# A weighted sum of two expert outputs: each partition owns 128 tokens in a row, weights in one DMA, one last store

## The chip, the cores and the metric

The kernel runs on one core of one Trainium2 chip. The metric is device time in microseconds of one execution; lower is better. The core has a vector engine (VectorE, DVE in the profile), a scalar engine (ScalarE, ACT), two more engines that matter little here, and a sequencer that only issues transfers (SyncE, SP). Transfers between main memory (HBM) and on-chip memory (SBUF, 128 partitions) run on 16 DMA engines, which are fed by one queue for SP (q1 in the profile) and one for ACT (q10).

## The reference

For 16 x 1024 = 16384 tokens there are the outputs of two experts, 512 numbers each, and two weights. The result is their weighted sum:

```python
batch, seq, hidden, n_experts, k = 16, 1024, 512, 8, 2
# expert_outputs: (batch, seq, k, hidden), combine_weights: (batch, seq, k), float32
weights = combine_weights[..., np.newaxis]
return np.sum(expert_outputs * weights, axis=2).astype(np.float32)
```

That is 64 MiB to read, 32 MiB to write and 128 KiB of weights.

## The kernel before

Every partition gets 128 tokens, worked on in 16 groups (the loop over `g`) of J = 8 tokens. A group's input tile `et` is 128 partitions x 8 tokens x 1024 numbers: 32 KB for a partition, 4 MB in all. Six such tiles exist (`bufs=6`), so the load of group g + 6 reuses the memory of group g, once that group's store has read it.

Which tokens a partition gets is decided by the helper `rows`. The first 120 x 128 tokens are dealt so that partition p has 120 tokens in a row. The last 8 x 128 tokens are dealt so that partition p has 8 in a row. So in groups 0 to 14 the rows of two neighbouring partitions lie 120 tokens apart in memory (480 KB for the input, 240 KB for the output), and group 15 is one contiguous block (rows 32 KB and 16 KB apart).

The weights lie in the tile `wt`. They are loaded by two DMAs on ACT's queue (line 53): one for the 120 tokens, one for the 8. Line 58 is a small ScalarE instruction that loads its function table early.

In each group:
- Line 64 (SP) loads `et`. All 16 loads are issued from SP, in order.
- In groups 0 to 14, line 69 (VectorE) multiplies the tile by the weights in place, line 70 adds the two halves into `ot` (the first half of the same tile), and line 71 (ACT's queue) stores `ot`, 16 KB for a partition in one run.
- In group 15 the work is done token by token, to be short at the end: line 78 (ScalarE) scales the first expert's output, line 81 (VectorE) multiplies the second by its weight and adds. After every second token line 89 (SP) stores two tokens of every partition. These are four stores, with 4 KB for a partition each.

The order in an engine is fixed when the kernel is built, by a scheduler that moves a few instructions. VectorE's last four line-69 and line-70 instructions come in pairs, and two line-78 instructions stand in ACT's queue ahead of the last two stores of line 71. Transfers signal their end through eight semaphores, used in turn. So a transfer may also wait until an older one with the same semaphore has landed. In the kernel before, the fifth and the sixth load wait in this way for the two weight transfers.

Of the kernel before, what the change touches and what calls it, by code (L numbers as in the profile page):

```python
# [1 line left out]

# [4 lines left out]


@with_exitstack
def kernel(  # L10
    ctx: ExitStack,
    tc: tile.TileContext,
    expert_outputs: bass.AP,
    combine_weights: bass.AP,
    out: bass.AP,
):

    nc = tc.nc  # L20
    b, s, k, h = expert_outputs.shape
    assert k == 2
    n = b * s
    P = nc.NUM_PARTITIONS
    per = n // P
    assert per * P == n
    J = 8
    main = per - J
    eo = expert_outputs.rearrange("b s k h -> (b s) (k h)")
    cw = combine_weights.rearrange("b s k -> (b s) k")  # L30
    o = out.rearrange("b s h -> (b s) h")

    def rows(x):

        a = x[0 : P * main, :].rearrange("(p t) f -> p t f", p=P)
        b = x[P * main : n, :].rearrange("(p t) f -> p t f", p=P)
        return lambda t, c: a[:, t : t + c, :] if t < main else b[:, t - main : t - main + c, :]

    eo, cw, o = rows(eo), rows(cw), rows(o)

    dt = mybir.dt.float32
    mult = mybir.AluOpType.mult
    add = mybir.AluOpType.add
    copy = mybir.ActivationFunctionType.Copy

    last = per // J - 1

    wpool = ctx.enter_context(tc.tile_pool(name="w", bufs=1))
    ipool = ctx.enter_context(tc.tile_pool(name="in", bufs=6))

    wt = wpool.tile([P, per * k], dt)
    for t, c in ((0, main), (main, J)):
        nc.scalar.dma_start(
            out=wt[:, k * t : k * (t + c)].rearrange("p (t k) -> p t k", k=k), in_=cw(t, c)
        )

    warm = wpool.tile([P, 1], dt)
    nc.scalar.activation(out=warm, in_=nc.const_aps.tensor(1.0, (P, 1), dt), func=copy)  # L58

    for g in range(per // J):  # L60
        et = ipool.tile([P, J, k * h], dt)

        ot = et.rearrange("p j f -> p (j f)")[:, 0 : J * h].rearrange("p (j f) -> p j f", f=h)
        nc.sync.dma_start(out=et, in_=eo(g * J, J))  # L64
        if g < last:

            wb = wt[:, g * J * k : (g + 1) * J * k].unsqueeze(2).to_broadcast([P, J * k, h])
            ek = et.rearrange("p j (k h) -> p (j k) h", k=k)
            nc.vector.tensor_tensor(out=ek, in0=ek, in1=wb, op=mult)  # L69
            nc.vector.tensor_tensor(out=ot, in0=et[:, :, 0:h], in1=et[:, :, h : 2 * h], op=add)  # L70
            nc.scalar.dma_start(out=o(g * J, J), in_=ot)  # L71
            continue


        for c0 in range(0, J, 2):
            for i in range(c0, c0 + 2):
                t = g * J + i
                nc.scalar.activation(  # L78
                    out=et[:, i, 0:h], in_=et[:, i, 0:h], func=copy, scale=wt[:, 2 * t : 2 * t + 1]
                )  # L80
                nc.vector.scalar_tensor_tensor(  # L81
                    out=ot[:, i, :],
                    in0=et[:, i, h : 2 * h],
                    scalar=wt[:, 2 * t + 1 : 2 * t + 2],
                    in1=et[:, i, 0:h],
                    op0=mult,
                    op1=add,
                )
            nc.sync.dma_start(out=o(g * J + c0, 2), in_=ot[:, c0 : c0 + 2, :])


# [1 line left out]
_INS = ['expert_outputs', 'combine_weights']  # L93
_OUTS = [((16, 1024, 512), 'float32')]


# [23 lines left out]
```

## Time and profile before

| what | value |
|---|---|
| median of 4 runs | 240.79 us (240.65 to 240.85) |
| the profiled execution | 240.84 us, of which 238.7 us are the profile's span |
| VectorE busy | 201.3 us (84%), 38 instructions |
| ScalarE busy | 6.6 us (3%), 10 instructions |
| moved | 100.80 MB in 5328 packets, mean 422 GB/s |
| line 69, multiply | 15 times 8689 ns |
| line 70, add | 15 times 4423 ns |
| line 64, load | 16 of 4096 KB, median 47.2 us from issue to landing |
| line 71, store | 15 of 2048 KB, median 24.8 us |
| line 89, last stores | 4 of 512 KB, median 8.0 us |
| line 53, weights | 120 KB, 12.6 us; 8 KB, 22.0 us |

How to read it: a transfer's time from issue to landing holds the time that it stands in its queue behind others. In the rows of a DMA queue, the share is the time that its packets took, as a part of the time of all 16 engines in the stretch shown. A row's bytes over that time therefore give the speed of one engine while it works for that queue. MB are millions of bytes there.

### The profile page before, as it was taken

How to read it: one execution, taken by the hardware profiler on the slowest of the kernel's cores; microseconds unless marked ns; L12 is line 12 of the kernel's file. 1: busy time of each engine (PE TensorE's matmuls, PEld its weight loads, DVE VectorE, ACT ScalarE, POOL GpSimd, SP SyncE). 2: the span in 40 equal slices, each digit the busy share in tenths (PEclk: the TensorE clock that was granted, in tenths of full speed). 3: DMA queues.
4: the chain of work that ended last, by engine and by line, in shares of the span. 5: the costliest groups of instructions: out<-in, count | busy, mean ns of one | idle time of the engine just before them, and what ended most of it. 6: DMA issues, size and time to landing. Idle time of an engine off the chain costs nothing.

```text
span 238.7 us, 177 instructions
## 1 busy us (share of the span) xinstructions
DVE 201.3 (84%) x38; ACT 6.6 (3%) x10; POOL 0.2 (0%) x4
## 2 busy tenths in 40 slices
DVE  0079999999999998979979799797918999899940
ACT  2000000000000000000000000000000000000620
POOL 0000000000000000000000000000000000000000
DMA  7999989999999999999999999999999999999997
GB/s 269 452 443 440 428 349 437 412 439 483 434 401 417 428 428 439 437 475 406 423 412 483 395 437 442 439 406 428 483 393 439 442 437 401 439 478 395 398 403 300
DMA packets 5328, 100.80 MB, mean 422 GB/s; under 512 B 720, under 2 KB 848, under 8 KB 1360
## 3 DMA queue, kind: packets, MB, share of 16 engines
q1 hardware_dynamic: 2880, 69.21, 67.9%
q10 hardware_dynamic: 2448, 31.59, 31.0%
HBM read 67.24 MB, written 33.55 MB: 422 GB/s over the span
## 4 chain that ended last, share of the span: by engine, by line
DMA 65%; DVE 29%; ACT 1%; ACTq 0%; DVEq 0%; issue 0%; SPq 0%
DMA et<-in_expert_outputs_dram 39%; DMA out_dram<-et 21%; DVE et L69 18%; DVE et L70 10%; DMA wt<-in_combine_weights_dram 5%; ACT et L78 1%; DVE et L81 1%; DVEq L115 0%; ACTq L115 0%; ACTq L71 0%; SPq L64 0%; DVEq L81 0%
## 5 line engine op out<-in xcount | busy, mean ns | idle before, releaser
L69 DVE TENSOR_TENSOR et<-et,wt 128x8192 f32<-128x8192 f32 x15 | 130.3, 8689 | 27.8 <-DMA et<-in_expert_outputs_dram 14.4
L70 DVE TENSOR_TENSOR et<-et 128x4096 f32<-128x4096 f32 x15 | 66.2, 4423 | 0.4
L78 ACT ACTIVATE et<-et,wt 128x512 f32<-128x512 f32 x8 | 5.1, 710 | 220.0 <-DMA et<-in_expert_outputs_dram 218.1
L81 DVE SCALAR_TENSOR_TENSOR et<-et,wt 128x512 f32<-128x512 f32 x8 | 5.6, 748 | 0.2
L58 ACT ACT_TABLE_LOAD x1 | 1.3, 1283 | 1.7 <-PEq L104 1.7
L58 ACT ACTIVATE warm<-const-float32-1.0 128x1 f32<-128x1 f32 x1 | 0.2, 202 | 0.0
L104 POOL MEMSET const-bfloat16-1.0<- 128x1 bf16 x1 | 0.1, 101 | 0.0
L104 POOL MEMSET const-uint8-127<- 128x1 uint8 x1 | 0.1, 101 | 0.0
L104 POOL MEMSET const-float32-0.0<- 128x1 f32 x1 | 0.1, 98 | 0.2 <-issue 0.2
L104 POOL MEMSET const-float32-1.0<- 128x1 f32 x1 | 0.1, 98 | 0.0
## 6 DMA issues: line engine op xcount, KB each, us to landing
et<-in_expert_outputs_dram SPq DMA_DIRECT2D x16, 4096.0 KB, 47.2
out_dram<-et ACTq DMA_DIRECT2D x15, 2048.0 KB, 24.8
out_dram<-et SPq DMA_DIRECT2D x4, 512.0 KB, 8.0
wt<-in_combine_weights_dram ACTq DMA_DIRECT2D x1, 120.0 KB, 12.6
wt<-in_combine_weights_dram ACTq DMA_DIRECT2D x1, 8.0 KB, 22.0
```

Source lines behind the costliest of these rows:

```text
L58: nc.scalar.activation(out=warm, in_=nc.const_aps.tensor(1.0, (P, 1), dt), func=copy)
L69: nc.vector.tensor_tensor(out=ek, in0=ek, in1=wb, op=mult)
L70: nc.vector.tensor_tensor(out=ot, in0=et[:, :, 0:h], in1=et[:, :, h : 2 * h], op=add)
L78: nc.scalar.activation(out=et[:, i, 0:h], in_=et[:, i, 0:h], func=copy, scale=wt[:, 2 * t : 2 * t + 1])
L81: nc.vector.scalar_tensor_tensor(out=ot[:, i, :], in0=et[:, i, h : 2 * h], scalar=wt[:, 2 * t + 1 : 2 * t + 2], in1=et[:, i, 0:h], op0=mul ...
L104: nc = _bacc.Bacc("TRN2", target_bir_lowering=False, num_devices=1)
```

## The change

Partition p now owns tokens 128 p to 128 p + 127 for all 16 groups. Rows of neighbouring partitions lie 128 tokens apart in every load and store (512 KB for the input, 256 KB for the output). The weights come in one DMA, 1024 bytes for a partition, issued from SP ahead of the loads. Group 15 stores its eight tokens with one DMA after the last of them. The arithmetic is the same, instruction for instruction. In the built kernel, VectorE's order and that of ScalarE's arithmetic are as before; ACT's queue has two transfers fewer at its start; SP has one more at its start and one instead of four at its end. SP's first five loads now wait for nothing, and the sixth waits for the landing of load 0.

```diff
-    main = per - J
-    eo = expert_outputs.rearrange("b s k h -> (b s) (k h)")
-    cw = combine_weights.rearrange("b s k -> (b s) k")
-    o = out.rearrange("b s h -> (b s) h")
-
-    def rows(x):
-
-        a = x[0 : P * main, :].rearrange("(p t) f -> p t f", p=P)
-        b = x[P * main : n, :].rearrange("(p t) f -> p t f", p=P)
-        return lambda t, c: a[:, t : t + c, :] if t < main else b[:, t - main : t - main + c, :]
-
-    eo, cw, o = rows(eo), rows(cw), rows(o)
+    eo = expert_outputs.rearrange("b s k h -> (b s) (k h)").rearrange("(p t) f -> p t f", p=P)
+    cw = combine_weights.rearrange("b s k -> (b s) k").rearrange("(p t) k -> p (t k)", p=P)
+    o = out.rearrange("b s h -> (b s) h").rearrange("(p t) f -> p t f", p=P)
...
-    for t, c in ((0, main), (main, J)):
-        nc.scalar.dma_start(
-            out=wt[:, k * t : k * (t + c)].rearrange("p (t k) -> p t k", k=k), in_=cw(t, c)
-        )
+
+    nc.sync.dma_start(out=wt, in_=cw)
...
-        nc.sync.dma_start(out=et, in_=eo(g * J, J))
+        nc.sync.dma_start(out=et, in_=eo[:, g * J : (g + 1) * J, :])
...
-            nc.scalar.dma_start(out=o(g * J, J), in_=ot)
+            nc.scalar.dma_start(out=o[:, g * J : (g + 1) * J, :], in_=ot)
...
-        for c0 in range(0, J, 2):
-            for i in range(c0, c0 + 2):
...
-            nc.sync.dma_start(out=o(g * J + c0, 2), in_=ot[:, c0 : c0 + 2, :])
+        for i in range(J):
...
+        nc.sync.dma_start(out=o[:, g * J : (g + 1) * J, :], in_=ot)
```

More of the change, by code (lines that the diff above doesn't have):

```diff
@@ L70 @@
             nc.vector.tensor_tensor(out=ot, in0=et[:, :, 0:h], in1=et[:, :, h : 2 * h], op=add)
-            nc.scalar.dma_start(out=o(g * J, J), in_=ot)
+            nc.scalar.dma_start(out=o[:, g * J : (g + 1) * J, :], in_=ot)
             continue
-        for c0 in range(0, J, 2):
-            for i in range(c0, c0 + 2):
[L77 to L89, printed above, removed]
+        for i in range(J):
+            t = g * J + i
+            nc.scalar.activation(
+                out=et[:, i, 0:h], in_=et[:, i, 0:h], func=copy, scale=wt[:, 2 * t : 2 * t + 1]
+            )
+            nc.vector.scalar_tensor_tensor(
+                out=ot[:, i, :],
+                in0=et[:, i, h : 2 * h],
+                scalar=wt[:, 2 * t + 1 : 2 * t + 2],
+                in1=et[:, i, 0:h],
+                op0=mult,
+                op1=add,
+            )
+        nc.sync.dma_start(out=o[:, g * J : (g + 1) * J, :], in_=ot)
 _INS = ['expert_outputs', 'combine_weights']
```

## The prediction, made before the changed kernel was run

> **What bounds the kernel now.** I read the page from part 2 downwards: which resource is never free, then how fast it works in each stage, and last what the end of the span waits for. First the slices and the queues of the page:
>
> ```profile
> DVE  0079999999999998979979799797918999899940
> ...
> DMA  7999989999999999999999999999999999999997
> ...
> q1 hardware_dynamic: 2880, 69.21, 67.9%
> q10 hardware_dynamic: 2448, 31.59, 31.0%
> HBM read 67.24 MB, written 33.55 MB: 422 GB/s over the span
> ```
>
> The DMA row is full from the second slice to the last but one. The two queues (q1 is fed by SP, with loads and the last stores; q10 by ACT, with weights and the other stores) take 67.9% + 31.0% = 98.9% of all 16 engines' time. VectorE has 201.3 us of work in 238.7 us, so 37 us of slack. The time is therefore bytes over the speed of one DMA engine, plus a short head and tail. A change counts only if it alters the speed at which an engine moves a packet, or leaves engines empty.
>
> So the second view is the DMA view cut to stretches. In each row: packets, MB, share of 16 engines. First the middle, 62 to 192 us (loads at 480 KB pitch, stores at 240 KB):
>
> ```profile
> q1 hardware_dynamic: 1296, 37.75, 67.2%
> q10 hardware_dynamic: 1280, 18.61, 33.4%
> ```
>
> One engine moves 37.75 MB / (0.672 x 16 x 130 us) = 27.0 GB/s on loads and 18.61 / (0.334 x 2080) = 26.8 GB/s on stores. Then 205 to 220 us, where q1 carries the last load, whose 128 rows of 32 KB lie one behind the other:
>
> ```profile
> q1 hardware_dynamic: 154, 4.19, 64.8%
> ```
>
> That is 4.19 / (0.648 x 240) = 26.9 GB/s, the same speed. The third stretch, 22 to 32 us, is the one where loads are slower:
>
> ```profile
> q1 hardware_dynamic: 137, 3.96, 99.0%
> ```
>
> 3.96 / (0.990 x 160) = 25.0 GB/s, at an unchanged pitch of 480 KB. So the engines can lose 8% without any change of layout. The trace doesn't say why. The fourth, 231 to 237 us, is the tail with the four last stores in 4 KB packets:
>
> ```profile
> q1 hardware_dynamic: 524, 1.95, 81.4%
> ```
>
> 1.95 / (0.814 x 96) = 25.0 GB/s. These packets cost 7% more than the 16 KB ones.
>
> Third view: the timeline of the end.
>
> ```profile
> 221.29 0.34 ACTq L71 DMA_DIRECT2D out_dram<-et  x1
> ...
> 223.94 5.77 DVE L81 SCALAR_TENSOR_TENSOR et<-et,wt 128x512 f32<-128x512 f32 x8
> 224.06 0.34 ACTq L71 DMA_DIRECT2D out_dram<-et  x1
> ...
> 225.57 4.50 SPq L89 DMA_DIRECT2D out_dram<-et  x4
> ```
>
> When the last load has landed (221.2 us), the stores of groups 13 and 14 are still to be moved, then the four quarters of group 15. The end is a queue of writes, not arithmetic.
>
> **Part 1, the pitch.** Loads go from rows 480 KB apart to rows 512 KB apart, stores from 240 to 256 KB, weights from 960 to 1024 bytes. Bytes, packet sizes (32 KB and 16 KB) and the number of large DMAs stay. Only the starting addresses of the 128 rows move, and with them which parts of memory the 16 engines ask at one moment. No row of this trace shows a strided tile at a power-of-two pitch: the last load has a pitch of 32 KB, but its tile is one contiguous 4 MB block. So bounds. The low end is zero: both the nearest pitch (480 KB, 27.0 GB/s) and the contiguous tile (26.9 GB/s) run at one speed. A gain is excluded for this term, since no stretch exceeds 27.0. The high end is the slowest stretch. All loads at 25.0 GB/s take 67.11 MB / (16 x 25.0) = 167.8 us instead of 67.11 / (16 x 27.0) = 155.3 us, +12.4 us; the same 8% on the stores' 33.55 / (16 x 26.8) = 78.2 us is +6.3 us. Both: +18.7 us. I take a third of the way for the loads, +4.1 us, since the two rows that are like in kind stand at the low end, while address bits that are all alike in 128 rows can only make engines meet more often. Stores are spaced half as far: half of that share, +1.0 us. Sum +5.1 us, with both ends kept.
>
> The Trainium skill ("DMA: Bandwidth & Descriptors", section "Latency and other measured facts") has a row that speaks against this change: copies with a row pitch of 512 KiB reached 207 GB/s per direction, where a padded pitch reached 214, and far less at 2 and 4 MiB; it calls the mechanism an inference. By its ratio (an estimate from that page) 3.4% would fall on the loads, 5.3 us, or on loads and stores, 7.9 us. No run here shows it.
>
> **Part 2, the weights.** Removed: two issues on ACT (0.90 us together, at 0.72 us) and 128 packets of 64 bytes. Added: one issue on SP ahead of all 16 loads. SP's issues take 0.33 us (median), the first or worst 0.77 us, so load 0 starts up to 0.33 to 0.77 us later. In that gap the engines move the weights, 8 packets each. Packets of 960 bytes took 44 ns (112 of them were 3.1% of 160 us in the stretch from 2 to 12 us), so 0.35 us that they no longer take between the loads' packets. Net 0 to +0.4 us of empty engines, or a gain of 0.1 us from the small packets gone. I take +0.1 us. VectorE's start hardly moves: it waited for the weights until 13.39 us, but load 0, which must land too, was 12.5 us from its issue at 0.73. Earlier or later by 0.5 us doesn't count, for the DMA engines are full then. ACT's table load moves up, and its next need is at 221 us.
>
> Semaphore waits move as well. Before, SP's fifth and sixth loads waited for the two weight transfers (19.9 us in the view of SP's waits); after, five loads go at once and the sixth waits for load 0. Cost nothing either way, as four loads are 16.8 MB, 39 us of work in the queue. If that cover were gone, each such wait would be empty engines.
>
> **Part 3, the last store.** Four issues on SP become one, of 128 packets of 16 KB. Transfer: 2.10 MB / (16 x 25.0) = 5.24 us becomes 2.10 / (16 x 26.8) = 4.89 us, -0.35 us. Against it, the store now waits for all eight L81 instructions (end 229.71 us) instead of the first pair. What hides this: the stores of groups 13 and 14, 4.19 MB or 9.8 us, which start no earlier than 221.3 + 0.7 (from the issue of load 0 at 0.73 us to the first bytes near 1.4 us) = 222.0 us and last until 231.8. The single store can move at 229.75 + 0.7 = 230.5 us. Cover 1.3 us; cost 0. Behind the waiting SP nothing is queued. If the cover is gone, the engines are empty for at most the 4 us between the first pair's store and the last.
>
> The Trainium skill ("SBUF — State Buffer", "The DMA setup-cost knee") charges about 2 us to every DMA. Three fewer would by that estimate save 6 us; the quarters here overlap, and 0.35 us is what their rows allow.
>
> **Sum**, against the profiled execution of 240.84 us (span 238.7 and 2.1 around it; the median of the runs, 240.79, is the same within 0.05): 240.84 + 5.1 + 0.1 - 0.35 = 245.7 us.
>
> **The rivals.**
> - **The pitch costs nothing.** For it: the rows at 27.0 and 26.9 GB/s, which hint that an engine's own limit binds. Against it: 16 engines now walk rows with identical low address bits. 240.84 - 0.25 = 240.6 us, no change. Chance 0.14.
> - **Faster: the slow early stretch goes away.** The slow rows at 22 to 32 us lie where the sixth load had been issued late, behind the second weight transfer. If that made them slow, one tile returns from 25.0 to 27.0 GB/s: 4.19 / (16 x 25.0) - 4.19 / (16 x 27.0) = 0.78 us. With a free pitch: 240.84 - 0.25 - 0.78 = 239.8 us. It decides only if the pitch costs under about 0.5 us. Against it: the slowness begins some 5 us after that issue, and nothing of the queue had run dry. Chance 0.12.
> - **The tail runs dry.** A free pitch, but the cover of 1.3 us is missing: up to 4 us, say 242 us. Chance 0.04.
>
> **How the numbers follow.** A slower load stream, between +0.8 us and the upper bound, has 0.70, with 245.7 us as its value. About 0.2% (0.48 us) is what a measurement of this kernel can tell from no change. Slower: 0.70 + 0.04 = 0.74; within 0.2%: 0.14; faster: 0.12. The range starts at 240.3 us, so as to hold the free pitch and leave out most of the faster case (about 0.1), and ends at 252 us, which is +11.4 us for the pitch, about 60% of the way to its upper bound; I leave about 0.1 above. Alone, the likeliest case reaches from 241.5 to 252 us.
>
> **What would show it.** Right: in the stretch 62 to 192 us the loads' packets take more than the 27.0 GB/s row says (near 26.3), DMA still full, and VectorE's idle time before L69's successor grows by some 5 us. At the end one store with 16 KB packets follows two others without a gap, and the chain ends about 9 us after the last L81's start. Wrong: the rows stand at 27.0 GB/s (pitch free), or go below 25.0 (the bound fails), or empty DMA slices show at the head or the tail, or stores slow while loads don't.

## The result: 0.11% above the kernel before

The changed kernel takes 240.92 us, the kernel before 240.75 us over all its runs. The ratio is 1.0011 (interval 1.0006 to 1.0016), so it is slower by about 0.26 us (0.17 us by the medians), half of what the prediction called the limit of no change. The forecast was 245.7 us. The profiled execution took 241.53 us, of which 239.5 us are the span. The other runs go from 240.55 to 241.64 us, so the profiled execution is not a typical one; it lies 0.6 us above the median.

The page of the changed kernel, the same rows as before:

```profile
DMA  7999999999999999999999999999999999999897
...
q1 hardware_dynamic: 2592, 69.34, 67.9%
q10 hardware_dynamic: 2160, 31.46, 30.7%
HBM read 67.24 MB, written 33.55 MB: 421 GB/s over the span
```

DMA is as full as before (98.6% of the engines' time against 98.9%). If the pitch had cost what was forecast, the same bytes would have taken more time. The DMA view cut to 62 to 192 us tells whether an engine got slower (packets, MB, share of 16 engines):

```profile
q1 hardware_dynamic: 1289, 37.52, 66.8%
q10 hardware_dynamic: 1282, 18.71, 33.6%
```

37.52 / (0.668 x 2080) = 27.0 GB/s on loads and 18.71 / (0.336 x 2080) = 26.8 on stores: the speeds of before, to the digit. By the packets of the traces, one of 32 KB took 1.213 us on the mean from 60 to 200 us, in both kernels. The early slow stretch, 22 to 32 us, is still there:

```profile
q1 hardware_dynamic: 132, 3.80, 97.5%
```

3.80 / (0.975 x 160) = 24.4 GB/s, against 25.0 before. The end, in the timeline:

```profile
222.54 0.72 ACT L64 ACTIVATE et<-et,wt 128x512 f32<-128x512 f32 x1 [220.32 <-DMA et<-in_expert_outputs_dram]
222.60 0.34 ACTq L59 DMA_DIRECT2D out_dram<-et  x1
...
225.28 5.77 DVE L67 SCALAR_TENSOR_TENSOR et<-et,wt 128x512 f32<-128x512 f32 x8
225.39 0.34 ACTq L59 DMA_DIRECT2D out_dram<-et  x1
...
231.08 0.35 SPq L75 DMA_DIRECT2D out_dram<-et  x1
```

The one last store is issued when the eighth sum is done, and the store of group 14 still occupies the engines then (its last part ends at 233.5 us). The beginning is later. In the view of waits, VectorE's first multiply waited 13.4 us for the weights; now it waits for load 0, and the longest wait is 14.3 us. Before, then after:

```profile
DVE et L69 <- DMA wt<-in_combine_weights_dram: 13.4, 1, 13.4
```

```profile
DVE et L57 <- DMA et<-in_expert_outputs_dram: 29.1, 9, 14.3
```

So VectorE starts 0.9 us later in these two executions, while the whole change costs about 0.26 us by the ratio. Something was lost at the head and something won at the tail.

The packets of the two traces, added up over the 16 engines, say where. The last byte moves at 238.4 us instead of 237.3. Until 13 us the engines stand empty for 0.4 us longer, and the first packets of the loads together take 0.2 us longer. At 28 to 33 us, where the first store joins, the slow packets cost 1.2 us instead of 0.8. The single last store wins 0.3 us. And there is a gap that the prediction doesn't have: between 215 and 228 us the engines are empty for 0.7 us, where it was 0.3. Group 13's store (the one issued at 222.60) stands in ACT's queue behind the first line-64 instruction, which waits for the last load. The last engine ends its part of that load at 222.18 us. The engines end the store of group 12, one after another, from 222.27 us on, and the first packets of group 13's store come at 223.45. In the kernel before the three times are 220.84, 221.71 and 222.13. Since this execution took 0.6 us more than the median, its trace doesn't tell how much of these losses a typical one has.

### The profile page after: what moved, and what is told of

Its sections match the earlier page's. It is cut to its first block, busy times and chain, and to the rows that moved or that the text cites. A ratio compares the mean times of both kernels' runs of the same rounds, so it can differ in the third digit from the quotient of the medians.

```text
span 239.5 us, 169 instructions
## 1 busy us (share of the span) xinstructions
DVE 201.3 (84%) x38; ACT 6.6 (3%) x10; POOL 0.2 (0%) x4
## 4 chain that ended last, share of the span: by engine, by line
DMA 65%; DVE 29%; ACT 1%; ACTq 0%; DVEq 0%; issue 0%; SPq 0%
DMA et<-in_expert_outputs_dram 43%; DMA out_dram<-et 22%; DVE et L57 18%; DVE et L58 10%; ACT et L64 1%; DVE et L67 1%; DVEq L101 0%; ACTq L101 0%; SPq L43 0%; ACTq L59 0%; SPq L52 0%; DVEq L67 0%; DVEq L57 0%
```

## The experiments

**One part at a time.** Two theories. A: the pitch is free, and the small loss is the weights' place at the head less the saving of the one store. B: the pitch itself costs the little that was lost. Four kernels take the change apart: the pitch alone in the kernel before; the changed kernel with its weights back on ACT; the last store alone in the kernel before; the changed kernel with four last stores.

```diff
# e1, in the kernel before
-        a = x[0 : P * main, :].rearrange("(p t) f -> p t f", p=P)
-        b = x[P * main : n, :].rearrange("(p t) f -> p t f", p=P)
-        return lambda t, c: a[:, t : t + c, :] if t < main else ...
+        a = x.rearrange("(p t) f -> p t f", p=P)
+        return lambda t, c: a[:, t : t + c, :]
# e2, in the changed kernel
-    nc.sync.dma_start(out=wt, in_=cw)
+    nc.scalar.dma_start(out=wt, in_=cw)
# e3, in the kernel before
-            nc.sync.dma_start(out=o(g * J + c0, 2), in_=ot[:, c0 : c0 + 2, :])
+        nc.sync.dma_start(out=o(g * J, J), in_=ot)
# e4, in the changed kernel
-        nc.sync.dma_start(out=o[:, g * J : (g + 1) * J, :], in_=ot)
+            if i % 2:
+                nc.sync.dma_start(out=o[:, t - 1 : t + 1, :], in_=ot[:, i - 1 : i + 1, :])
```

> The kernel before with the 512 KB pitch alone (weights still two transfers on ACT's queue, 960 and 64 bytes for a partition, four last stores). Theory A (the pitch is free; the +0.17 us of the whole change is a later head, about +0.5 us, less a shorter tail, about -0.35 us): 240.7 to 240.9 us, ratio 1.000, and 27.0 GB/s for an engine on loads from 62 to 192 us. Theory B (the pitch costs the little that was lost, the other parts cancel): 241.0 to 241.5 us, ratio 1.001 to 1.003. The prediction's own term would be 245.8 us.

> The changed kernel with its one weight transfer back on ACT's queue, beside load 0 instead of ahead of it. Theory A: the head gets its 0.5 us back and the tail keeps its gain, 240.3 to 240.5 us, ratio 0.998; load 0's first packets start at about 1.5 us instead of 2.0. Theory B: 240.9 us or more, as the pitch stays.

> The kernel before with one last store of 8 tokens instead of four of 2. Theory A: 128 packets of 16 KB instead of 512 of 4 KB save 0.35 us and nothing runs dry, 240.4 us, ratio 0.9985. Theory B, or a tail that waits: 240.75 us or more.

> The changed kernel with four last stores of 2 tokens again. Theory A: the saving of the tail is lost, 241.25 us, ratio 1.002. Theory B: 240.9 us, as the changed kernel, since the store would then be worth nothing.

| kernel | median, us | ratio to the kernel before, interval |
|---|---|---|
| e1, pitch alone | 241.16 | 1.0022 (1.0012 to 1.0033) |
| e2, changed, weights on ACT | 240.64 | 0.9992 (0.9983 to 1.0001) |
| e3, before, one last store | 240.20 | 0.9981 (0.9972 to 0.9990) |
| e4, changed, four last stores | 241.29 | 1.0030 (1.0018 to 1.0041) |

Neither theory holds alone. The pitch costs 0.22%, about 0.5 us (against A). The one store saves 0.19%, about 0.46 us (against B). The weights ahead of the loads cost 0.19% by the changed kernel against e2, and 0.08% by e4 against e1; the first difference is uncertain by about 0.1%, the second by about 0.15%. The traces show the place: load 0's first packet starts at 1.75 us in e2 and at 2.23 in the changed kernel. Three parts of 0.2 to 0.5 us, one of the other sign, make the 0.26 us.

And yet e1's loads run at full speed from 62 to 192 us:

```profile
q1 hardware_dynamic: 1294, 37.68, 67.1%
```

37.68 / (0.671 x 2080) = 27.0 GB/s. So where do its 0.5 us go?

**Where the pitch costs.** The table of stretches gives the mean over the first 11.6 us in which data moves (last number, GB/s). The kernel before, then e1:

```profile
1.40:13.00 11.60, 0.00 (x0) 1.49 (x2) 0.00 (x0) 1.00 1.03 417
```

```profile
1.40:13.00 11.60, 0.00 (x0) 1.49 (x2) 0.00 (x0) 1.00 1.01 400
```

17 GB/s less for 11.6 us are 0.2 MB, which take 0.46 us at the 432 GB/s of the full engines. That is rough, since the row counts whole packets by their starts, and 0.2 MB are six packets. The packets of the trace show it finer. The first engine begins load 0 at 1.73 us in the kernel before and 1.74 in e1; the last begins at 2.33 and at 2.64. The first packet takes 1.86 us on the mean before and 1.96 in e1, and the first of load 1 1.21 and 1.38; the others up to 28 us take 1.21 to 1.23. So load 1 ends 0.50 us later in e1, on the mean of the engines, and load 8 is still 0.41 us late: the loss of about 0.5 us comes at the head and doesn't grow. The engines also end their parts of a load further apart. This is the time between the first and the last engine's completion of one load, and the mean time of completion, worked out from the completion packets of the profiled executions:

```
us from the first to the last engine's end of    load 0   load 2   load 8   mean end of load 1   load 8
before                                            0.44     0.37     0.37       22.30             121.23
e3, before with one last store                    0.46     0.46     0.46       22.35             121.31
e1, pitch alone                                   0.93     1.78     1.78       22.80             121.64
changed kernel                                    1.13     1.59     1.59       22.83             121.97
e5, 512 KB pitch from load 4 on                   0.32     0.29     0.31       22.38             121.23
e6, 512 KB pitch in loads 0 to 3                  0.85     0.92     0.92       22.58             121.54
```

Theory C: the pitch costs where the engines start together; it sets them apart once, and from then on they don't hinder each other. Theory D: it costs a little all along. Two kernels with mixed pitches tell them apart (some loads read other tokens than they should):

```diff
+    wide = eo.rearrange("(p t) f -> p t f", p=P)
...
-        nc.sync.dma_start(out=et, in_=eo(g * J, J))
+        nc.sync.dma_start(out=et, in_=wide[:, g * J : (g + 1) * J, :] if g >= 4 else eo(g * J, J))   # e5; g < 4 in e6
```

> The kernel before, but the loads of groups 4 to 15 are addressed at 512 KB pitch and those of groups 0 to 3 at 480 KB as before (so some tokens are read for others; stores and weights as before). Theory C (the pitch costs only where 16 engines start together, in the first 32 us; it sets them apart in time and the distance stays until the end): as the kernel before, 240.6 to 240.9 us, and the 16 parts of a load land within 0.4 us of each other all the way. Theory D (the pitch costs a little all along): 12 of 16 loads are wide, so 241.0 to 241.2 us, and the distance grows with every load.

> The reverse: loads of groups 0 to 3 at 512 KB pitch, those of groups 4 to 15 as before (some tokens are read for others). Theory C: as with the pitch alone, 241.0 to 241.3 us, and the 16 parts of a load land 1 to 2 us apart from the first loads on. Theory D: 4 of 16 loads are wide, so 240.8 to 240.95 us, with a distance that doesn't grow after group 3.

e5, with 12 of 16 loads wide, is at 1.0004 (0.9994 to 1.0013): no loss that can be measured. e6, with only the first four wide, is at 1.0035 (1.0022 to 1.0048), 241.45 us, even above C's expectation of 241.0 to 241.3. The first stretch agrees, e5 first, then e6:

```profile
1.40:13.00 11.60, 0.00 (x0) 1.49 (x2) 0.00 (x0) 1.00 1.04 417
```

```profile
1.40:13.00 11.60, 0.00 (x0) 1.49 (x2) 0.00 (x0) 1.00 1.01 406
```

D is out: the interval of e6, from 241.26 us up, lies above D's 240.95, and in e5 the wide loads hardly spread the engines and come no later than before (121.23 us for load 8 in both). So the loss belongs to the first four loads, as C says, and by the completion times to their first packets. Two points of C aren't borne out. The parts of e6's loads end 0.85 to 0.92 us apart and not 1 to 2. And the distance isn't what makes later wide loads free: in e5 the engines stay within 0.3 to 0.4 us of each other, and the wide loads cost nothing. The trace of e6 is of an execution of 240.50 us. Its other four took 241.41 to 241.68 us, and no trace shows where they lost more than the 0.3 us that this one is late at the head. Why wide addresses make the first packets later (a shared part of memory that several engines ask at once is the obvious guess) was not shown.

**Is there a pitch that costs all along?** Two ladders, read by stretches. In e9 the stores go to a scratch tensor at 512 KB, then 1 MB, then 2 MB pitch. In e10 four tiles are copied to a scratch tensor and loaded from there at 1 and 2 MB.

```diff
# e9
-            nc.scalar.dma_start(out=o[:, g * J : (g + 1) * J, :], in_=ot)
+            m = (1 << 17, 1 << 18, 1 << 19)[g // 5]
+            w = g * J * h
+            lad = big[0 : P * m].rearrange("(p c) -> p c", p=P)[:, w : w + J * h]
+            nc.scalar.dma_start(out=lad.rearrange("p (j f) -> p j f", f=h), in_=ot)
# e10
+        src = lad(17 + g // 4, g % 4) if 4 <= g < 12 else eo[:, g * J : (g + 1) * J, :]
```

> The changed kernel whose stores of groups 0 to 14 go to a scratch tensor instead of the output: groups 0 to 4 at a pitch of 512 KB, 5 to 9 at 1 MB, 10 to 14 at 2 MB. If a power-of-two pitch costs nothing at these sizes, an engine moves 26.8 GB/s on stores in all three stretches. If the term that the prediction charged exists but begins above 512 KB, the stretch at 2 MB is slower by 10% or more (by the skill's row, 164 against 207, about 21%), and the one at 1 MB lies between.

> Four tiles are first copied to a scratch tensor (8 stores of 4 MB, at 1 and 2 MB pitch). Then the changed kernel runs with the loads of groups 0 to 3 and 12 to 15 at 512 KB pitch, groups 4 to 7 from the scratch at 1 MB, groups 8 to 11 at 2 MB (so these give other tokens' sums). If pitch is free: 27.0 GB/s for an engine on loads in all stretches. If the term begins above 512 KB: 27.0 at 512 KB, lower at 1 MB, and 24 GB/s or less at 2 MB.

e9, DMA view from 107 to 139 us, as the stores at 1 MB begin, and from 140 to 181 us, when they have been running for a while:

```profile
q1 hardware_dynamic: 284, 8.36, 72.0%
q10 hardware_dynamic: 276, 4.00, 29.2%
```

```profile
q1 hardware_dynamic: 407, 11.96, 67.8%
q10 hardware_dynamic: 399, 5.85, 33.3%
```

Loads drop to 8.36 / (0.720 x 512) = 22.7 GB/s in the first and are back at 11.96 / (0.678 x 656) = 26.9 in the second, at the same pitch. The stores themselves keep 26.8 in both. At 2 MB, 182 to 226 us, it is again the loads beside them that are slower, at 12.85 / (0.709 x 704) = 25.7 GB/s, and the stores keep 26.8:

```profile
q1 hardware_dynamic: 448, 12.85, 70.9%
q10 hardware_dynamic: 369, 5.47, 29.0%
```

e10, loads at 1 MB pitch from 185 to 230 us, then at 2 MB from 231 to 288 us:

```profile
q1 hardware_dynamic: 428, 12.65, 67.6%
```

```profile
q1 hardware_dynamic: 552, 16.35, 67.0%
```

12.65 / (0.676 x 720) = 26.0 GB/s at 1 MB, and 16.35 / (0.670 x 912) = 26.8 GB/s at 2 MB: next to nothing lost there, with four times the pitch of the change. At the end of e9 stores stand alone at 2 MB pitch, 229 to 241 us:

```profile
q10 hardware_dynamic: 281, 4.19, 97.5%
```

4.19 / (0.975 x 192) = 22.4 GB/s, 16% below the 26.8 that they have beside loads. Standing alone isn't the reason, for in the kernel before the stores that are alone from 221 to 226 us move 2.08 / (0.987 x 80) = 26.3 GB/s:

```profile
q10 hardware_dynamic: 143, 2.08, 98.7%
```

So wider pitches do cost, in some stretches and not in others: on the loads for a time after the stores' pattern changed, little on loads at 2 MB in a steady stream, most on stores alone at 2 MB. e9 fits neither of its two cases, as the stores at 2 MB are slower only where they stand alone. It took 250.07 us in its one run, so these stretches add up. e10 (372.19 us) does more work, and its time isn't comparable. The Trainium skill ("DMA: Bandwidth & Descriptors", section "Latency and other measured facts") gives 207 and 164 GB/s per direction for copies at pitches of 512 KiB and 2 MiB, where 214 is the full rate. The 22.4 GB/s here agrees with it in direction. The 27.0 of the loads at 512 KB and the 26.8 of loads and of stores at 2 MB in a mixed stream don't, and the measurement decides for this kernel.

**The slow stretch at 28 to 32 us.** It is in both traces and was one of the prediction's rivals. Is it the first write as such (e7: a small store near the start, on top of e3), or does it follow the first full store (e8: that store held back)?

```diff
# e7
+    first = wpool.tile([P, 64], dt)
+    nc.gpsimd.memset(first, 0.0)
+    scratch = nc.dram_tensor("scratch", [P, 64], dt, kind="Internal").ap()
+    nc.scalar.dma_start(out=scratch, in_=first)
# e8
+            if g == 0:
+                held = ot
+                continue
+            if g == 1:
+                nc.vector.tensor_copy(out=held[:, 0, 0:1], in_=ot[:, 0, 0:1])
+                nc.scalar.dma_start(out=o(0, J), in_=held)
             nc.scalar.dma_start(out=o(g * J, J), in_=ot)
```

> The kernel before with one last store, and a store of 128 x 256 bytes to a scratch tensor issued from ACT's queue near the start. If the slow packets at 28 to 32 us come from the first write to memory as such, they are gone there (0.7 us of all engines) and the time is 239.5 to 239.9 us. If they come from the first full store beside a full load stream, or from something at that time, they stay and the time is 240.2 to 240.4 us.

> The kernel before with its first store held back until group 1 is done, about 13 us later (a copy of one number for a partition from group 1 into group 0's output makes it wait, so one output number in a row is wrong). If the slow packets follow the first store, they move from 28 to 32 us to about 41 to 45 us. If they belong to the loads or the time, they stay at 28 to 32 us.

In e7 the slow packets stay, at 30 to 34 us. Its time is 1.0013 (1.0005 to 1.0021), slower than e3 without the small store, which nobody expected. The view of its timeline shows the place:

```profile
221.92 0.72 ACT L83 ACTIVATE et<-et,wt 128x512 f32<-128x512 f32 x1 [218.77 <-DMA out_dram<-et]
222.03 0.34 ACTq L76 DMA_DIRECT2D out_dram<-et  x1
```

It is the gap that the changed kernel's trace has. The view names a store as what released ACT's first work on group 15, but the semaphore for which ACT's queue waits there signals loads alone: the last load lands at 221.83 us, 0.9 us later than in e3. Group 13's store, queued behind on ACT, is issued at 222.03 us (221.00 in e3), its first packets come at 222.87, and the engines had ended the store of group 12 between 221.50 and 222.11. The engines are empty for 1.1 us there; in e3 they are not. Why one more small transfer near the start makes the last load land later was not shown.

In e8 the slow packets move to 41 to 46 us, with the store, and are weaker: the 32 KB packets from 20 to 60 us take 0.16 us for each engine more than 1.213 us apiece, against 0.76 in the kernel before. Its single run took 239.68 us. To see whether that is a gain, the hold was built so that the result stays the same (zero times a number of group 1 is added) and put on e3 and on the changed kernel:

```diff
+            if g == 1:
+                nc.vector.scalar_tensor_tensor(
+                    out=held[:, 0, 0:1], in0=ot[:, 0, 0:1], scalar=0.0, in1=held[:, 0, 0:1], op0=mult, op1=add
+                )
+                nc.scalar.dma_start(out=o(0, J), in_=held)
```

> The kernel before with one last store and its first store held back: group 0's store waits for group 1's sums (a VectorE instruction on one number for a partition that adds zero times a number of group 1 makes the wait, and the result stays the same). If the single run of e8 (239.68 us) showed a gain of the late first store, and the last store adds its 0.45 us: 239.1 to 239.5 us, ratio 0.994, slow packets moved to about 41 to 45 us. If e8 was a lucky run: 240.1 to 240.3 us, ratio 0.998, as with one last store alone.

> The same hold in the changed kernel. If the cost of the pitch lies in the first loads (theory C) and the joining of the first store is a cost of its own, then the hold gains the same as in the kernel before, about 0.7 us: 240.1 to 240.4 us, and the 16 parts of a load still land more than 1 us apart. If the pitch costs only when the stores join: more gain, 239.7 us or less, with 0.5 us between the parts.

e11 is at 239.57 us, 0.9947 (0.9935 to 0.9960): faster than both kernels, and 0.34% below e3. e12 is at 240.44 us, 0.9985 (0.9976 to 0.9994), 0.26% below the changed kernel. Both are a little above what was expected. The gain is the same within the intervals, and the parts of a load still end 1.23 us apart in e12. The slow packets cost 0.34 us in e11 (0.80 in e3) and 0.39 in e12 (1.17 in the changed kernel). So the joining of the first store is a cost of its own, apart from the pitch. The hold has a second effect: the last load lands some 5 us before the store of group 12 ends, so no gap arises there. In e3 there was none to close; in e12 part of the gain may come from that. The DMA view from 27 to 33 us shows the loads where the first store joins, the kernel before, and then e11, in which it is held back:

```profile
q1 hardware_dynamic: 63, 2.06, 92.3%
q10 hardware_dynamic: 16, 0.26, 10.2%
```

```profile
q1 hardware_dynamic: 95, 2.59, 100.0%
```

2.06 / (0.923 x 96) = 23.2 GB/s before, 2.59 / 96 = 27.0 in e11, where no store has begun. Why the loads slow down when the first store joins, and why less so 13 us later, stays open.

e11 also shows that the distance between the engines doesn't slow them. At 480 KB pitch its parts end 0.43 us apart up to load 3, and 1.66 us from load 6 on, after the held store has joined. That is as far as in e1, and e11 is the fastest of all kernels that were run more than once.

## Why the prediction was wrong, step by step

- **The bound** was right: DMA engines at 27.0 and 26.8 GB/s, full in both kernels but for the head, the very end and the gap before group 13's store.
- **Part 1, the pitch, is the step that failed.** It took a speed between 27.0 and 25.0 GB/s and charged it on every byte: +5.1 us. The runs showed 27.0 and 26.8 GB/s at the new pitch, which is the sign that the prediction had named for a free pitch. Its own rows stood at 27.0 and 26.9, and the 25.0 belonged to something else, the first store's joining, as e8 and e11 show. The sign was right, the size ten times too big: e1 measured +0.22%, 0.5 us, paid once at the head. The two rows of the trace at one speed for two pitches hinted that the engine's own limit binds. The prediction wrote this down for the rival and gave it 0.14.
- **Part 2, the weights**: +0.1 us forecast, with 0 to 0.4 as ends. Measured +0.2 us (e4 against e1) to +0.46 us (changed kernel against e2), from the middle of that span to just above its end.
- **Part 3, the last store**: -0.35 us forecast, -0.46 us (0.19%) measured in e3. The cover held: the store was issued at 231.08 us and the engines were busy with group 14's store until 233.5. The gap before group 13's store, 0.3 us in the trace before and 0.7 in the trace after, had no term.
- **The rivals.** "The pitch costs nothing" (240.6 us, no change) came nearest and is right for the rate; it missed the 0.5 us at the head. "The early slow stretch goes away" fell: it stayed at 24.4 GB/s although the sixth load no longer waited for weights. "The tail runs dry" didn't happen at the last store, where it was expected.
- **The sum** with measured terms: +0.5 + 0.2 to 0.46 - 0.46 = +0.2 to +0.5 us. Measured: +0.26 us. That this is so near to no change is luck: the saving of the store happened to cancel most of two losses. The measured 240.92 us lies within the stated range only because the range's low end was put there for the free pitch; the likeliest case began at 241.5 us.

## What to carry to other kernels

When transfers bind, first ask whether each engine already moves its packets at one speed under different layouts. If it does, look for a layout's cost at the start and where the pattern changes, and count it once and not on every byte, as here at 512 KB. An average speed from one slow stretch is no price for another cause. Look too at what the last load releases: a store that waits behind it leaves the engines empty when the older stores end first (0.3 to 1.1 us here). And a releaser that a view names is to be held against the time at which it was done.

## What the runs showed of the hardware that was not expected

- The 16 engines keep the distance that a start or the first store's joining gives them: 0.37 us in the kernel before, 1.78 in e1 and 1.59 in the changed kernel, unchanged from about 34 us on over 140 us; 1.66 in e11 from load 6 on. The distance goes with no loss of speed.
- The first packets of a store come 0.84 us after its issue (222.03 to 222.87 us in e7, 221.29 to 222.13 in the kernel before), so a store issued when the older ones are nearly done leaves the engines empty.
- After a change to stores at 1 MB pitch, loads beside them ran at 22.7 GB/s and recovered to 26.9 GB/s by themselves (e9, one run).
- Loads lose speed when the first store joins (23.2 GB/s from 27 to 33 us), and holding that store back by 13 us gains 0.26 to 0.34%.
